# One matrix of the token mixer, v's 1,024 columns, as seven Strassen block products among u's chunks

## The chip, the cores and the metric

The kernel runs on one core of one Trainium2 chip. The metric is the device time of one execution in microseconds (us), lower being better. Five engines matter here: TensorE (PE, with its weight loads PEld), VectorE (DVE), ScalarE (ACT), GpSimd (POOL) and SyncE (SP), whose queue issues most loads.

## What is computed

Two layers of a decoder trunk over 256 tokens of width 1,024, each an FFN, a mixer and a second FFN, all in float32. The part that matters:

```python
def _mixer(x, ...):
    z = x @ w_in
    u, v, q, k, val, gates = jnp.split(z, SPLITS, axis=-1)
    u = jax.nn.gelu(u, approximate=False)
    v = jax.nn.gelu(v, approximate=False)
    h_a = _chunked_sgu(u, v, sgu_ln_g, sgu_ln_b, sgu_w, sgu_b)
    ...                                   # q, k, val -> h_b, by differential attention
    g = jax.nn.sigmoid(gates.reshape(bsz, seq, N_BRANCH, D_MODEL) + gate_b)
    m = g[:, :, 0] * (h_a @ w_branch[0]) + g[:, :, 1] * (h_b @ w_branch[1])
    return m @ w_out

def _chunked_sgu(u, v, g, b, w_s, b_s):
    v = _layernorm(v, g, b)
    ...                                   # 8 groups of 128 columns, chunks of 128 tokens
    s = jnp.einsum('gtr,bnrgc->bntgc', w, vb) + b_s.T[None, None, :, :, None]
    return u * s.reshape(bsz, seq, SGU_WIDTH)
```

So v is one product of x (256 x 1,024) and a 1,024 x 1,024 matrix, followed by a GELU and a layer norm over its columns.

## The kernel before

**Precision by pieces.** Each float32 matrix is split into a high part (ACT copies it into the reduced format float32r) and a low part (DVE subtracts the high part from the original). A product is three passes on PE: high x high, low weights x high, high weights x low. `split` does this for activations; `stream` and `pieces` do it for weights, 128x1024 at a time. The high and low parts of weights live in two pools, `hi` and `lo`, of eight 128x1024 slots each (`HL`). The raw weights arrive by `fetch`, one DMA of 1 MB on SP's queue, into four `raw` slots.

**Two shapes of product.** `gemm_a2` (lines 295 and 302) gives transposed results: weights are stationary, and the high and low parts of x lie side by side as a moving operand of 512 columns; u, q, k and half of the gates use it, one chunk of 256 columns at a time, two weight pieces each. `gemm_b` and `gemm_b2` (through `rows_b` and `three`, line 283) give token rows: x is stationary, a weight piece holds two of the eight k blocks for 512 columns, and the two token blocks of 128 are two PSUM banks. A piece costs six matmuls of 512 columns per token block. val, v and half of the gates use it.

**The mixer's order on PE.** PE's order is that in which the program is written (PE is scheduled by hand); the other engines' instructions are ordered by a scheduler according to priority and readiness, in order once issued. val (`gemm_b2`, during the last steps of the norm before), four pairs of q and k, gates (rows and columns, twice), u's chunks 0 and 1, v in two halves of 512 columns, u's chunks 2 and 3, the branch of attention (`branch_rows(1)`, `branch_columns(1)`), the branch of the gating unit (`branch_rows(0)`, `branch_columns(0)`), and w_out.

**Work beside it.** Attention (`attend`), `settle` (v's norm) and `spatial` (the 128x128 position mixing, a few PE matmuls each, then DVE and ACT) are generators. `beside(task, delay)` starts one after so many beats; `beat(w)` counts them along PE's program: a chunk of `gemm_a2` is 2 beats, a product of 12 matmuls is 1, a half of `gemm_b` is 4. POOL does attention's copies and reciprocal roots, and issues the loads of constants, `wsT` and `bsb` for `spatial` among them.

**Strassen in the FFNs.** The FFNs have such products already: `strassen_sums` makes four sums of blocks of x out of the rows that the norm leaves in `norm.rows` (in place), and splits each; `seven` and `gemm_seven` run seven products of 128x512 by 512x512. Sums of weights come from `plus` (a DVE add, line 359) and `gather` (a DMA on POOL's queue that adds to what is in SBUF, line 353). One product is this, with `x` a sum of x or a block of it:

```python
def product(ps, x, w, start, stop):
    for k in range(4):
        hi, lo = (v[:, k % 2 * 512 : k % 2 * 512 + 512] for v in w[k // 2])
        for n, (y, o) in enumerate(((hi, 0), (lo, 0), (hi, 1))):
            PE.matmul(ps, x[o](k), y, ...)                 # line 376
        beat(0.25)
```

While `line[2]` is set, every weight split and every `plus` is queued behind the one before it on its engine, in the program's order.

Of the kernel before, what the change touches and what calls it, by code (L numbers as in the profile page):

```python
# [12 lines left out]
F32R = mybir.dt.float32r  # L13
# [41 lines left out]
def trunk(ctx, tc, x, xT, w13a, w13b, w2, wb, wqk, wu, wg, wgr, wbr, wbrr, wo, gateb, gatebr, sgug, sgub, sguwT, sgubias, lam, diffg,  # L55
# [48 lines left out]
    def sm(s, n, dtype=F32, bufs=2):  # L104
        return small.tile([P, n], dtype, tag=f"{s}{n}", name=name(s), bufs=bufs)
# [139 lines left out]
    def split(hi, lo, src, eng=V, after=(None, None)):  # L245
        with behind(after[0]):
            a = A.activation(hi, src, AF.Copy).ins  # L247
        with behind(after[1]):
            return a, eng.tensor_tensor(out=lo, in0=src, in1=hi.bitcast(F32), op=ALU.subtract).ins  # L249
# [329 lines left out]
    class Norm:  # L579
# [166 lines left out]
        def close(self):  # L746
# [3 lines left out]
            return self  # L750

    def ffn(l, f, i, norm, last=False):
        xh, xl = parts(both)
# [80 lines left out]

        def strassen_sums(to, made, v11, v21, v12, v22, apart=1):
            to[:] = [tuple(lambda k, v=v: v[:, k * P : (k + 1) * P] for v in m) for m in made]
            for n, (out, a, b, op) in ((0, (v22, v21, v22, ALU.subtract)), (2, (v21, v11, v21, ALU.subtract)),
                                       (1, (v11, v22, v11, ALU.subtract)), (3, (v12, v12, v11, ALU.add))):
                V.tensor_tensor(out=out, in0=a, in1=b, op=op)
                if n in (2, 3):  # L840
                    yield apart
            for n, out in ((0, v22), (2, v21), (1, v11), (3, v12)):
                split(*made[n], out)
                yield apart

        def seven(src, x_sums):

            x11, x12, x22 = (tuple(lambda k, o=o, t=t, h=h: x_cat[h][:, k, o + t * P : o + (t + 1) * P] for o in (0, T))
                             for t, h in ((0, 0), (0, 1), (1, 1)))
            (w11, w21), (w12, w22) = ([v[:, o : o + CH] for o in (0, CH)] for v in src)  # L850
# [92 lines left out]
    def mixer(l, i, norm):  # L943
# [9 lines left out]

        gemm_b2([wb[l, VAL_, 0], wb[l, VAL_, 1]], xh, xl, got_val, norm=norm)

        hb = slots("hb", 2 * KT, F32R)
# [169 lines left out]

        u_part((0, 1))
        vg = [act.tile([P, 2, 512], F32, tag="val", name=name("vg"), bufs=2) for _ in range(NT)]
        vst = [sm("vst", 12, bufs=2) for _ in range(NT)]
        for h in range(2):  # L1130
            def got_v(t, ps, c, n):
                A.activation(vg[t][:, h], ps, AF.Gelu)
                V.bn_stats(out=vst[t][:, h * 6 : h * 6 + 6], in_=vg[t][:, h])
            gemm_b(wb[l, V_, h], KT, xh, xl, got_v)
        def settle():
            for t in range(NT):
                mv = sm("mv", 2)
                V.bn_aggr(out=mv, in_=vst[t])
                r = rsqrt(mv[:, 1:2], EPS)
                for h in range(2):  # L1140
                    s = slice(h * 512, h * 512 + 512)
                    V.scalar_tensor_tensor(out=vg[t][:, h], in0=vg[t][:, h], scalar=mv[:, 0:1], in1=g_bc[:, s],
                                            op0=ALU.subtract, op1=ALU.mult)
                    V.scalar_tensor_tensor(out=vg[t][:, h], in0=vg[t][:, h], scalar=r, in1=b_bc[:, s],
                                            op0=ALU.mult, op1=ALU.add)
                    yield 1

# [29 lines left out]

        beside(settle(), 2.6)
        for gp in range(GROUPS // 2):
            beside(spatial(gp), 7.4 + 1.1 * gp)  # L1180
        u_part((2, 3))

# [149 lines left out]
```

## Time and profile before

| | |
|---|---|
| median of 3 runs | 1189.68 us (1189.35 to 1190.64) |
| profiled execution | 1189.92 us, span of its instructions 1188.2 us |
| granted TensorE clock | 1.000 |
| PE busy | 1180.8 us, 99%, 5771 matmuls |
| DVE, ACT, POOL busy | 85%, 70%, 25% |
| DMA | 276.15 MB, mean 232 GB/s |

How to read the profile's rows: L283 is line 283 of the kernel before; an instruction is given as output<-inputs by the names of tiles, with partitions x elements. A group shows its count, the time in which at least one of it ran, the mean duration of one in ns, and the idle time ahead of it with what ended it. A timeline's row has start and length in us. Matmuls overlap, so their pitch (start to start) counts and not their duration. In the table of windows an engine's column is its busy time in the window, with its count of instructions.

### The profile page before, as it was taken

What the parts mean: (1) busy time and instruction counts of PE and PEld (TensorE: products, weight loads), DVE (VectorE), ACT (ScalarE), POOL (GpSimd) and SP (SyncE); (2) the same over time, 40 slices, a digit from 0 to 9 for tenths busy, and PEclk for the clock granted to TensorE, in tenths of its full rate; (3) what the DMA queues carried; (4) which work ended last, traced back from release to release, by engine and by line L of the source; (5) the groups of instructions that cost most, each with busy time, mean ns of one, the idle gap of its engine ahead of it and who ended that gap; (6) DMA issues with size and microseconds to landing.
All of it is one profiled execution on the core that took longest, in us unless ns stands there. A gap on an engine that the chain in (4) does not pass through costs nothing.

```text
span 1188.2 us, 16675 instructions
## 1 busy us (share of the span) xinstructions
PE 1180.8 (99%) x5771; PEld 993.6 (84%) x5771; DVE 1010.2 (85%) x1558; ACT 828.5 (70%) x1418; POOL 297.3 (25%) x356
## 2 busy tenths in 40 slices
PE   9999999999999999999999999999999999999998
PEld 7888888888888888888888888888888888888887
DVE  6889989888688989889899889888965989988895
ACT  6688667559955677886567877576788556679761
POOL 1211301247420220071020061004564112102510
PEclk9999999999999999999999999999999999999999
DMA  9869976758865658689668699576666755886981
GB/s 348 277 205 265 304 267 206 264 191 222 256 205 181 222 184 274 197 290 263 226 215 267 184 300 275 186 289 233 211 204 207 255 177 172 256 250 211 291 231 36
DMA packets 129797, 276.15 MB, mean 232 GB/s; under 512 B 89088, under 2 KB 90160, under 8 KB 105648
## 3 DMA queue, kind: packets, MB, share of 16 engines
q1 hardware_dynamic: 121968, 248.80, 63.3%
q0 software_dynamic: 7312, 25.76, 9.3%
q8 instruction: 45, 0.74, 0.2%
q10 hardware_dynamic: 432, 0.52, 0.1%
q14 instruction: 40, 0.33, 0.1%
HBM read 249.10 MB, written 1.05 MB: 211 GB/s over the span
## 4 chain that ended last, share of the span: by engine, by line
PE 99%; DMA 1%; DVE 0%; ACT 0%; SPq 0%; issue 0%; ACTq 0%
PE bank L283 46%; PE bank L295 15%; PE sbank L376 12%; PE bank L405 10%; PE bank L302 8%; PE sbank L405 3%; PE bank L516 2%; PE sbank L991 1%; PE bank L376 1%; PE sbank L1047 1%; PE sbank L1165 1%; DMA raw<-in_w13b 1%; PE sbank L1045 0%; PE sbank L685 0%; PE sbank L664 0%; SPq L494 0%
## 5 line engine op out<-in xcount | busy, mean ns | idle before, releaser
L197 DVE TENSOR_TENSOR wlo<-raw,whi 128x1024 fp32r<-128x1024 f32 (+1 forms) x374 | 414.2, 1133 | 59.2 <-ACT whi L195 43.6
L195 ACT ACTIVATE whi<-raw 128x1024 fp32r<-128x1024 f32 (+1 forms) x378 | 353.0, 960 | 130.9 <-PE bank L283 43.7
L283 PE MATMUL bank<-whi,x 128*128 128x512 f32 x1224 | 386.3, 390 | 0.0
L283 PEld LDWEIGHTS bank<-whi,x 128*128 128x128 f32 x1224 | 229.8, 188 | 47.5
L283 PE MATMUL bank<-wlo,x 128*128 128x512 f32 x612 | 238.2, 389 | 0.0
L295 PE MATMUL bank<-x,whi 128*128 128x512 f32 x640 | 153.3, 391 | 0.0
L295 PEld LDWEIGHTS bank<-x,whi 128*128 128x128 f32 x640 | 118.2, 188 | 23.8
L283 PEld LDWEIGHTS bank<-wlo,x 128*128 128x128 f32 x612 | 114.9, 188 | 23.4
L249 DVE TENSOR_TENSOR wlo<-raw,whi 128x1024 fp32r<-128x1024 f32 (+1 forms) x96 | 109.8, 1161 | 16.7 <-ACT whi L247 7.8
L247 ACT ACTIVATE whi<-raw 128x1024 fp32r<-128x1024 f32 (+1 forms) x96 | 92.9, 984 | 41.6 <-DVE raw L359 23.4
L229 POOL COPY seven<-seven 128x512 uint16<-128x512 uint16 x16 | 63.7, 4041 | 108.4 <-ACT whi L195 54.6
L302 PEld LDWEIGHTS bank<-x,wlo 128*128 128x128 f32 x640 | 81.4, 191 | 2.9
L302 PE MATMUL bank<-x,wlo 128*128 128x256 f32 x640 | 82.6, 283 | 0.0
L405 PE MATMUL bank<-whi,hhi 128*128 128x512 f32 (+1 forms) x182 | 68.2, 374 | 0.0
L405 PE MATMUL bank<-whi,hlo 128*128 128x512 f32 (+1 forms) x182 | 67.9, 373 | 0.0
L405 PE MATMUL bank<-wlo,hhi 128*128 128x512 f32 (+1 forms) x182 | 67.9, 373 | 0.0
L967 POOL TENSOR_TENSOR swap<-swap,sin_t 128x512 f32<-128x512 f32 x16 | 27.5, 1716 | 100.6 <-DMA swap<-z 81.6
L728 POOL COPY nvia<-ntwo 128x256 uint16<-128x256 uint16 x20 | 9.6, 527 | 157.6 <-DMA ntwo<-nvia 107.6
L303 ACT ACTIVATE r<-bank 128x256 f32<-128x256 f32 x96 | 34.8, 372 | 16.6 <-PE bank L302 16.5
L359 DVE TENSOR_TENSOR raw<-raw,home 128x1024 f32<-128x1024 f32 x32 | 38.6, 1218 | 4.1 <-DMA home<-in_w13b 4.1
L376 PE MATMUL sbank<-whi,xhs 128*128 128x512 f32 x128 | 42.0, 389 | 0.0
L405 PEld LDWEIGHTS bank<-whi,hlo 128*128 128x128 f32 x182 | 34.3, 188 | 6.1
(283 smaller groups left out, 2154.7 us busy)
## 6 DMA issues: line engine op xcount, KB each, us to landing
raw<-in_w13b SPq DMA_DIRECT2D x68, 1024.0 KB, 5.5
raw<-in_w SPq DMA_DIRECT2D x32, 1024.0 KB, 6.4
raw<-in_wb SPq DMA_DIRECT2D x16, 1024.0 KB, 5.4
raw<-in_wqk SPq DMA_DIRECT2D x16, 1024.0 KB, 5.8
home<-in_w13b SPq DMA_DIRECT2D x16, 512.0 KB, 6.1
raw<-in_w13a SPq DMA_DIRECT2D x8, 1024.0 KB, 4.8
home<-in_w SPq DMA_DIRECT2D x16, 512.0 KB, 5.4
raw<-in_wgr SPq DMA_DIRECT2D x8, 1024.0 KB, 5.1
```

What stands on the lines that cost most here:

```text
L195: inline(A, A.activation(h, r, AF.Copy).ins)
L197: low = eng.tensor_tensor(out=w, in0=r, in1=h.bitcast(F32), op=ALU.subtract).ins
L229: eng.tensor_copy(out=o, in_=i)
L247: a = A.activation(hi, src, AF.Copy).ins
L249: return a, eng.tensor_tensor(out=lo, in0=src, in1=hi.bitcast(F32), op=ALU.subtract).ins
L283: PE.matmul(ps, xx, w, start=start and n == 0, stop=stop and n == 2)
L295: PE.matmul(b[-1], hi[:, k * P : (k + 1) * P], xc(k), start=k == 0, stop=False)
L302: PE.matmul(b[n][:, :T], lo[:, k * P : (k + 1) * P], xc(k)[:, :T], start=False, stop=k == KT - 1)
L303: emptied[0] = A.activation(r[:, s], b[n][:, T:], AF.Copy, scale=scale).ins
L359: inline(V, V.tensor_tensor(out=v, in0=v, in1=m, op=ALU.add).ins)
L376: PE.matmul(ps, x[o](k), y, start=start and k == n == 0, stop=stop and k == 3 and n == 2, skip_group_check=True)
L405: PE.matmul(q[c][t][:, :n] if o == 0 else more[:, :n], x(k, t), y, start=k == 8 and m == 0 and (c, t) != (1, 0), stop=k == FT - 1 and m == ...
```

## The change

v's 96 matmuls per mixer become seven products, 84 matmuls. A 2 x 2 grid of blocks is made of x (token block by half of k) and of the matrix (half of k by half of the columns). Seven products are run one after another in three side banks, `bx`, `bz` and `bq`; `bx` and `bz` go on adding up, and results of the blocks are read out between products (`got_v`). Five of the seven products take their weights from r1 and r2, two raw slots that hold w11 and w12 and then sums: one comes from `plus`, three from `gather`. The products are strung through u's four chunks: u 0, one product, u 1, one, u 2, two, u 3, three. The four sums of x are made right behind val and the norm, and their split parts take two `hi` and two `lo` slots until v ends. `settle` runs per token block, and it and `spatial` start behind the last product, with shorter delays, since no chunk of u comes after v any more. `strassen_sums` moves out of `ffn`, and the x blocks get a helper of their own; neither alters the FFNs.

```diff
@@ -749,6 +749,21 @@
                 x_cat = self.x
             return self
 
+    def strassen_sums(to, made, v11, v21, v12, v22, apart=1):
+        to[:] = [tuple(lambda k, v=v: v[:, k * P : (k + 1) * P] for v in m) for m in made]
+        for n, (out, a, b, op) in ((0, (v22, v21, v22, ALU.subtract)), (2, (v21, v11, v21, ALU.subtract)),
+                                   (1, (v11, v22, v11, ALU.subtract)), (3, (v12, v12, v11, ALU.add))):
+            V.tensor_tensor(out=out, in0=a, in1=b, op=op)
+            if n in (2, 3):
+                yield apart
+        for n, out in ((0, v22), (2, v21), (1, v11), (3, v12)):
+            split(*made[n], out)
+            yield apart
+
+    def x_blocks():
+        return (tuple(lambda k, o=o, t=t, h=h: x_cat[h][:, k, o + t * P : o + (t + 1) * P] for o in (0, T))
+                for t, h in ((0, 0), (0, 1), (1, 1)))
+
     def ffn(l, f, i, norm, last=False):
         xh, xl = parts(both)
         h_hi, h_lo = ([act.tile([P, 512], F32R, tag="slot", name=name(n)) for _ in range(FT // 2)] for n in ("hhi", "hlo"))
@@ -832,21 +847,9 @@
             made = [[home(v) for v in w] for w in (("main", "side"), ("side", "main"), ("main", "slot"), ("side", "slot"))]
             yield from strassen_sums(x_sums, made, t11, t21, t12, t22)
 
-        def strassen_sums(to, made, v11, v21, v12, v22, apart=1):
-            to[:] = [tuple(lambda k, v=v: v[:, k * P : (k + 1) * P] for v in m) for m in made]
-            for n, (out, a, b, op) in ((0, (v22, v21, v22, ALU.subtract)), (2, (v21, v11, v21, ALU.subtract)),
-                                       (1, (v11, v22, v11, ALU.subtract)), (3, (v12, v12, v11, ALU.add))):
-                V.tensor_tensor(out=out, in0=a, in1=b, op=op)
-                if n in (2, 3):
-                    yield apart
-            for n, out in ((0, v22), (2, v21), (1, v11), (3, v12)):
-                split(*made[n], out)
-                yield apart
-
         def seven(src, x_sums):
 
-            x11, x12, x22 = (tuple(lambda k, o=o, t=t, h=h: x_cat[h][:, k, o + t * P : o + (t + 1) * P] for o in (0, T))
-                             for t, h in ((0, 0), (0, 1), (1, 1)))
+            x11, x12, x22 = x_blocks()
             (w11, w21), (w12, w22) = ([v[:, o : o + CH] for o in (0, CH)] for v in src)
             bx, bz, bq = (side_bank() for _ in range(3))
             g0, v0, v1, g1 = (slots("seven", 2)[0] for _ in range(4))
@@ -952,6 +955,12 @@
                     A.activation(val[t][:, h], ps[h], AF.Copy)
 
         gemm_b2([wb[l, VAL_, 0], wb[l, VAL_, 1]], xh, xl, got_val, norm=norm)
+
+        x_sums = []
+        wide = [[p.tile([P, HC], F32R, tag=n, name=name("xhs")) for p, n in ((hi_pool, "hi"), (lo_pool, "lo"))] for _ in range(2)]
+        made = [[v[:, n % 2 * 512 : n % 2 * 512 + 512] for v in wide[n // 2]] for n in range(4)]
+        for _ in strassen_sums(x_sums, made, *(norm.rows[v] for v in ((0, 0), (1, 0), (0, 1), (1, 1)))):
+            pass
 
         hb = slots("hb", 2 * KT, F32R)
 
@@ -1124,26 +1133,67 @@
                 (_, uu), = gemm_a2([wu[l, gp]], both, lambda m: uu)
                 A.activation(uu, uu, AF.Gelu)
 
-        u_part((0, 1))
         vg = [act.tile([P, 2, 512], F32, tag="val", name=name("vg"), bufs=2) for _ in range(NT)]
         vst = [sm("vst", 12, bufs=2) for _ in range(NT)]
-        for h in range(2):
-            def got_v(t, ps, c, n):
-                A.activation(vg[t][:, h], ps, AF.Gelu)
+
+        def seven():
+
+            x11, x12, x22 = x_blocks()
+            (w11, w21), (w12, w22) = ([wb[l, V_, h][:, o : o + CH] for o in (0, CH)] for h in range(2))
+            bx, bz, bq = (side_bank() for _ in range(3))
+            cross = s512("cross")
+
+            def got_v(t, h, src=None):
+                A.activation(vg[t][:, h], vg[t][:, h] if src is None else src, AF.Gelu)
                 V.bn_stats(out=vst[t][:, h * 6 : h * 6 + 6], in_=vg[t][:, h])
-            gemm_b(wb[l, V_, h], KT, xh, xl, got_v)
-        def settle():
-            for t in range(NT):
-                mv = sm("mv", 2)
-                V.bn_aggr(out=mv, in_=vst[t])
-                r = rsqrt(mv[:, 1:2], EPS)
-                for h in range(2):
-                    s = slice(h * 512, h * 512 + 512)
-                    V.scalar_tensor_tensor(out=vg[t][:, h], in0=vg[t][:, h], scalar=mv[:, 0:1], in1=g_bc[:, s],
-                                            op0=ALU.subtract, op1=ALU.mult)
-                    V.scalar_tensor_tensor(out=vg[t][:, h], in0=vg[t][:, h], scalar=r, in1=b_bc[:, s],
-                                            op0=ALU.mult, op1=ALU.add)
-                    yield 1
+
+            product(bq, x12, pieces(fetch(w21)), True, True)
+            A.activation(cross, bq, AF.Copy)
+            yield
+            r1 = fetch(w11)
+            p1 = pieces(r1)
+            r2 = fetch(w12)
+            product(bx, x11, p1, True, False)
+            p1 = pieces(plus(r1, r2))
+            gather(r1, w22)
+            gather(r2, w22)
+            yield
+            V.tensor_tensor(out=vg[0][:, 0], in0=bx, in1=cross, op=ALU.add)
+            got_v(0, 0)
+            product(bz, x_sums[0], p1, True, False)
+            A.activation(vg[1][:, 1], bz, AF.Copy)
+            product(bx, x_sums[1], pieces(r1), False, False)
+            gather(r1, w21)
+            A.activation(vg[0][:, 1], bx, AF.Copy)
+            yield
+            product(bx, x_sums[2], pieces(r2), False, False)
+            V.tensor_tensor(out=vg[1][:, 1], in0=vg[1][:, 1], in1=bx, op=ALU.subtract)
+            got_v(1, 1)
+            product(bz, x_sums[3], pieces(fetch(w22)), False, True)
+            V.tensor_tensor(out=vg[0][:, 1], in0=bz, in1=vg[0][:, 1], op=ALU.subtract)
+            got_v(0, 1)
+            product(bx, x22, pieces(r1), False, True)
+            got_v(1, 0, bx)
+            yield
+
+        line[:] = None, None, True
+        products = seven()
+        for gp in range(GROUPS // 2):
+            u_part((gp,))
+            next(products)
+        line[:] = None, None, False
+
+        def settle(t):
+            mv = sm("mv", 2)
+            V.bn_aggr(out=mv, in_=vst[t])
+            r = rsqrt(mv[:, 1:2], EPS)
+            for h in range(2):
+                s = slice(h * 512, h * 512 + 512)
+                V.scalar_tensor_tensor(out=vg[t][:, h], in0=vg[t][:, h], scalar=mv[:, 0:1], in1=g_bc[:, s],
+                                        op0=ALU.subtract, op1=ALU.mult)
+                V.scalar_tensor_tensor(out=vg[t][:, h], in0=vg[t][:, h], scalar=r, in1=b_bc[:, s],
+                                        op0=ALU.mult, op1=ALU.add)
+                yield 0.8
 
         wsT, bsb = slots("wsT", 4), slots("bsb", 4)
         for h in range(2):
@@ -1175,10 +1225,10 @@
                 split(h[:, :T], h[:, T:], s1[:, j * T : (j + 1) * T])
             yield 0
 
-        beside(settle(), 2.6)
+        for t in range(NT):
+            beside(settle(t), 0.6 + t)
         for gp in range(GROUPS // 2):
-            beside(spatial(gp), 7.4 + 1.1 * gp)
-        u_part((2, 3))
+            beside(spatial(gp), 4.4 + 1.1 * gp)
 
         m_hi, m_lo, turned_rows = [], [], [None, None]
 
```

## The prediction

> **What bounds the kernel now.** I read the page first: busy time by engine, then the chain.
>
> ```profile
> span 1188.2 us, 16675 instructions
> PE 1180.8 (99%) x5771; PEld 993.6 (84%) x5771; DVE 1010.2 (85%) x1558; ACT 828.5 (70%) x1418; POOL 297.3 (25%) x356
> ```
> Busy PE alone proves little, since matmuls overlap. Hence the second view, the waits of PE:
>
> ```profile
> PE bank L516 <- ACT whi L247: 1.7, 1, 1.7
> PE sbank L528 <- DVE warm L524: 1.0, 1, 1.0
> PE sbank L664 <- ACT minus L662: 0.8, 1, 0.8
> ```
> These are all its waits: 3.5 us in 1188.2, two at the start, one in the last norm. In the mixers PE never waits, so a matmul taken out there shortens the run by its pitch, as long as everything else keeps up. Third view, the chain in order of time, around one Strassen product of the FFN, one u-like column group, and v's two stretches in layer 0:
>
> ```profile
> 152.38 2.72 PE sbank L376 x12
> ...
> 215.83 3.65 PE bank L295 x16
> 219.49 1.91 PE bank L302 x16
> ...
> 315.39 6.83 PE bank L283 x30
> 323.55 14.98 PE bank L283 x66
> ```
> A product is 2.72 us, so a matmul's pitch is 0.227. A column group (one u chunk) is 3.65 + 1.91 = 5.56. v is 6.83 + 14.98 = 21.81 for 96 matmuls.
>
> **The change part by part.** *PE.* v goes from 2 halves x 2 token blocks x 8 k x 3 passes = 96 matmuls to 7 products x 12 = 84: 7 x 2.72 = 19.04, a saving of 2.77 us per mixer, 5.5 us in two. Nothing is added on PE. [...]
>
> *Sums of x behind the norm.* Four adds and four splits of 128x512:
>
> ```profile
> L839 DVE TENSOR_TENSOR xf<-nvia,xf x3: 677/678/678, 450.7 to 1037.1; 128x512 f32<-128x512 f32 x3
> L247 ACT ACTIVATE xhs<-nvia x9: 619/634/638, 446.4 to 1042.7; 128x512 fp32r<-128x512 f32 x9
> L249 DVE TENSOR_TENSOR xhs<-nvia,xhs x9: 679/680/684, 453.1 to 1043.7; 128x512 fp32r<-128x512 f32 x9
> ```
> 8 x 0.68 = 5.4 us of DVE and 4 x 0.63 = 2.5 of ACT, once per mixer, off PE's path if the split weights are far enough ahead. How far they are, ACT's timeline against PE's shows (a split, and the first matmul that uses it):
>
> ```profile
> 264.79 2.94 ACT L195 ACTIVATE whi<-raw 128x1024 fp32r<-128x1024 f32 x3
> 277.61 0.45 PE L283 MATMUL bank<-whi,x 128*128 128x512 f32 x1
> ...
> 286.98 1.99 ACT L195 ACTIVATE whi<-raw 128x1024 fp32r<-128x1024 f32 x2
> 302.74 1.55 PE L295 MATMUL bank<-x,whi 128*128 128x512 f32 x6
> ...
> 356.55 1.06 ACT L195 ACTIVATE whi<-raw 128x1024 fp32r<-128x1024 f32 x1 [3.56 <-PE bank L283]
> 375.07 0.40 PE L283 MATMUL bank<-whi,ha 128*128 128x512 f32 x1
> ```
> Following the pieces in order, the first pair is the second gate's first piece (lead 12.8 us, about the lowest between the queries and the branches), the second u's first (15.8), the third the last branch's first, where ACT waits only for PE to free a slot (18.5). So 5.4 us of DVE is hidden, price 0; without cover it would be up to 5.4 per mixer.
>
> *Two of eight hi and lo slots held* from there until v ends. Six slots are four pieces ahead of the two in use. Pieces are used at 5.56/2 = 2.8 us each, so the lead falls by at most 2 x 2.8 = 5.6: 12.8 becomes 7.2 or more. Price 0, bounds 0 and a few us if ACT's bursts of attention grow longer than that.
>
> *The u and v stage.* Its busy time, the next stage's, and two FFN windows with products in them:
>
> ```profile
> 302.74:349.47 46.73, 46.73 (x251) 40.38 (x249) 34.36 (x61) 36.71 (x74) 16.77 (x41) 1.00 0.78 243
> 349.47:375.07 25.60, 25.60 (x147) 22.42 (x145) 22.44 (x40) 12.99 (x22) 0.00 (x0) 1.00 0.48 167
> ...
> 90.00:105.00 15.00, 15.00 (x68) 12.43 (x67) 15.00 (x18) 12.68 (x18) 0.00 (x0) 1.00 0.81 275
> 135.00:150.00 15.00, 15.00 (x68) 12.21 (x67) 15.00 (x16) 9.75 (x11) 1.82 (x3) 1.00 1.01 265
> ```
> (columns PE, PEld, DVE, ACT, POOL). The stage becomes 46.73 - 2.77 = 43.96. Added there, by these rows:
>
> ```profile
> L197 DVE TENSOR_TENSOR wlo<-raw,whi 128x1024 fp32r<-128x1024 f32 (+1 forms) x374 | 414.2, 1133 | 59.2 <-ACT whi L195 43.6
> L195 ACT ACTIVATE whi<-raw 128x1024 fp32r<-128x1024 f32 (+1 forms) x378 | 353.0, 960 | 130.9 <-PE bank L283 43.7
> L359 DVE TENSOR_TENSOR raw<-raw,home 128x1024 f32<-128x1024 f32 x32 | 38.6, 1218 | 4.1 <-DMA home<-in_w13b 4.1
> L1132 ACT ACTIVATE vg<-bank x8: 574/590/600, 325.4 to 925.0; 128x512 f32<-128x512 f32 x8
> L1172 DVE TENSOR_TENSOR sgu<-sgu,u x8: 681/688/693, 362.0 to 960.5; 128x512 f32<-128x512 f32 x8
> L1142 DVE SCALAR_TENSOR_TENSOR vg<-vg,mv,bc x8: 740/743/1049, 338.4 to 930.7; 128x512 f32<-128x512 f32 x8
> ```
> DVE: 6 more low halves (14 pieces for 8) x 1.11 = 6.6, two adds of r1 and r2 x 1.21 = 2.4, three joins of banks x 0.69 = 2.1; less the part of `settle` that leaves the stage, six of eight passes, 6 x 0.74 = 4.4. So 34.36 + 6.7 = 41.1 of 43.96, 93%. ACT: 6 x 0.93 + 3 copies x 0.59 = 7.4, so up to 44.1 of 43.96; but the stage now also splits ahead for the branches:
>
> ```profile
> 302.74:349.47 46.73, 18.17 (x18) 1.00 0.78 243
> ```
> 18 splits fall in it while u and v have 16, the net lead grown there. With six slots at most four pieces are ahead at either end, so 22 are due and none extra: 36.71 + 4 x 0.93 + 1.8 = 42.2, 96%. Tight, but the FFN windows show PE without a gap beside a DVE at 100%, with the same products and two slots lent. Price 0 to 0.3; bounds 0 and the second rival's.
>
> *The gathers.* Three accumulating loads of 1 MB on POOL's queue, six DMAs, ahead of the wsT and bias loads and among attention's POOL steps. Their cost now:
>
> ```profile
> L353 POOL DMA_DIRECT2D raw<-in_w13b x6: 850/872/917, 476.5 to 1064.2; - x6
> DMA to landing us min/median/max: 5.3/6.6/11.5
> ```
> Call T the end of the first product. Then u1 ends at T + 5.6, the w11 product at 8.3, u2 at 13.8, the next product at 16.6, and there the first gathered pieces are due. They follow this chain: the third pair of splits (its slots come free at T, two adds before it) ends about T + 4 to 6, as attention's steps interfere; second half issued 0.9 later; 6.6 to land; 0.9 + 1.1 to split: T + 13.5 to 15.5. It is due 1.4 after the product starts, T + 18. Margin 2.5 to 4.5 us. The second gather has T + 18 + 9.5 = 27.5 against 30.3 + 1.4. ACT's hi copy waits for the landing at its queue's head, and u3's copies (due T + 19.3) and u2's evacuation stand behind it. Price at the median landing 0; at 11.5 see the first rival.
>
> *Order after v.* `settle` and `spatial` now lie under the first branch only. Counted in beats, the last `spatial` falls right before the second branch's rows (before, one column group earlier). Its chain now:
>
> ```profile
> 371.30 1.06 PE L1165 MATMUL sbank<-wsT,vg 128*128 128x128 f32 x8
> 372.98 0.75 DVE L1170 TENSOR_TENSOR sgu<-sbank,bsb 128x256 f32<-128x256 f32 x2
> 375.31 0.42 DVE L249 TENSOR_TENSOR ha<-sgu,ha 128x256 fp32r<-128x256 f32 x1
> ```
> From the matmuls' end at 372.36 to the second low part at about 376.1: 3.7 us. It is used after three pieces of six matmuls, 18 x 0.227 = 4.1. It just fits; I take 0.3 per mixer, bounds 0 and 1. DVE in that window goes from 22.44 to 22.44 + 4.4 of 25.6, over 100%, but its pieces are about 14 ahead and lose at most 1.3 of that.
>
> Sum: -5.5 + 2 x 0.3 = -4.9 against the profiled execution's 1189.92 (span 1188.2 and 1.7 around it), which lies 0.24 above the median 1189.68: 1184.8 as a median. The forecast's own range is 1183.9 (no stall, 5.5 and 0.3 of spread) to 1187.2.
>
> **The rivals.** *Gathers land late.* With 11.5 us instead of 6.6 the first is ready at T + 18.4 to 20.4 against 18, the second as much later: 0.4 to 2.4 and some 0.5 more, about 2.4 per mixer: 1189.68 - 5.5 + 4.8 = 1189.0, no change. For it: attention's transposes run beside. Against: light traffic in v's stretch. The Trainium skill ("SBUF — State Buffer", section "SBUF: two separate sides") states that a load issued from POOL can starve for descriptors while DVE holds the port they share. By that rule a DVE at 93% would push landings to the upper row; the 6.6 median, found beside an FFN DVE at 90 to 100%, speaks against most of it.
>
> *ACT cannot fill its queue (slower).* In the stage ACT idles 46.73 - 36.71 = 10 us now. If half of that stays, since its head waits for gathers, freed slots and bank results, 44.1 + 5 = 49.1 us of queue stand against 43.96; the lead left at the end hides little with six slots, so some 4.5 us per mixer reach PE: 1189.68 - 5.5 + 9 = 1193.2. It turns into a loss from a stall over 2.8 per mixer, measurably from 4. For it: 96 to 100% of ACT in order, dependent on DVE, POOL and DMA. Against: FFN's products, and ACT had 12.8 to 18 us of lead here.
>
> *The change doesn't save PE time*, because products alternate between two banks: 1189.7. The x12 row at 2.72 speaks against it.
>
> **How the numbers follow.** Forecast 0.55; late gathers 0.16 (a quarter of it still faster); ACT 0.23; no saving 0.06. A measurement of this kernel tells about 0.2%, 2.4 us. Faster 0.58, same 0.18, slower 0.24. The range is 1183.9 to 1192.5, leaving out the worse half of the ACT case.
>
> **What would show it.** L283 loses 192 matmuls and L376 gains 168, each x12 still 2.72 us; PE's waits stay near 3.5 us; u's start to the first branch takes 44 us in place of 46.73. A PE wait on ACT whi or DVE wlo before the fourth product means gathers; one before the sixth or seventh product, with ACT busy throughout, means ACT; one on ha means `spatial`. I am wrong if PE waits over 3 us in a mixer anywhere.

## The result, and the profile after

The changed kernel takes 1236.93 us (1236.43 to 1237.46) against 1189.74 for the kernel before on the same chip: ratio 1.0396, interval 1.0378 to 1.0414. It is 47 us slower; the forecast was 5 us faster, and its range ended at 1192.5. The page of the changed kernel, as first shown for before:

```profile
span 1234.9 us, 16749 instructions
PE 1189.8 (96%) x5747; PEld 997.3 (81%) x5747; DVE 1047.5 (85%) x1596; ACT 841.9 (68%) x1444; POOL 313.0 (25%) x368
```

The 24 matmuls are gone (5771 to 5747), yet PE is busy for longer and idle 4% of the span. Its waits in the changed kernel (columns: total us, times, longest):

```profile
PE sbank L376 <- ACT d L1064: 14.5, 2, 7.5
PE sbank L1215 <- DVE vg L1194: 14.2, 3, 6.6
PE sbank L376 <- ACT vg L1167: 6.4, 2, 3.6
PE sbank L376 <- DVE vg L1170: 2.2, 2, 1.2
```

37.3 us in four new groups, all in the mixers: one wait ahead of the fourth product (L376), one ahead of the fifth (L1167 is the copy that empties bank `bx`), a small one ahead of the seventh, and one at `spatial` (L1215), which comes behind v. The windows of the changed kernel for u and v, and then the first branch, in the first mixer and the second (columns PE, PEld, DVE, ACT, POOL, granted clock, DMA share, GB/s):

```profile
303.62:363.44 59.82, 48.66 (x238) 40.78 (x237) 40.08 (x49) 41.97 (x83) 27.46 (x47) 0.91 0.86 225
363.44:397.97 34.53, 27.89 (x145) 23.90 (x144) 30.43 (x63) 16.44 (x24) 0.00 (x0) 0.90 0.51 183
912.20:972.05 59.85, 47.87 (x238) 40.26 (x237) 38.70 (x49) 41.07 (x81) 27.75 (x47) 0.91 0.84 224
972.05:1008.19 36.14, 28.59 (x146) 24.40 (x144) 31.31 (x62) 17.26 (x26) 0.00 (x0) 0.86 0.50 179
```

Before, these stages took 46.73 and 25.60 us in both mixers at a clock of 1.00. So u and v lost 13.1 us twice and the first branch 8.9 and 10.5: 45.7 of the 47. The clock column is new: it is below 1.00 in all four.

**Ahead of the fourth product.** The timeline of the changed kernel there, four engines together (in brackets stands how long the engine was idle before the instruction, and what ended that):

```profile
320.39 3.87 POOL L353 DMA_DIRECT2D raw<-in_wb  x4
...
330.99 0.39 PE L376 MATMUL sbank<-whi,xhs 128*128 128x512 f32 x1
...
332.54 1.06 ACT L247 ACTIVATE whi<-raw 128x1024 fp32r<-128x1024 f32 x1 [9.45 <-DMA raw<-in_wb]
333.63 1.23 DVE L249 TENSOR_TENSOR wlo<-raw,whi 128x1024 fp32r<-128x1024 f32 x1 [8.47 <-ACT whi L247]
335.37 1.06 ACT L247 ACTIVATE whi<-raw 128x1024 fp32r<-128x1024 f32 x1 [1.77 <-DMA raw<-in_wb]
336.46 1.23 DVE L249 TENSOR_TENSOR wlo<-raw,whi 128x1024 fp32r<-128x1024 f32 x1 [1.60 <-ACT whi L247]
337.61 0.68 DVE L1161 TENSOR_TENSOR vg<-sbank,cross 128x512 f32<-128x512 f32 x1
...
338.43 0.76 PE L376 MATMUL sbank<-whi,xhs 128*128 128x512 f32 x1 [7.06 <-ACT d L1064]
```

ACT stands 9.45 us at the head of its queue for a gathered piece, DVE 8.47 us for ACT. Behind DVE's two splits stands L1161, the add that reads `bx`, and the fourth product adds up in `bx`: PE restarts as soon as that add ends. The releaser that the profile names, ACT d, has nothing to do with it.

**Behind v.** The timeline of the changed kernel, DVE's row of v's norm and PE's at `spatial`:

```profile
368.52 0.15 DVE L255 TENSOR_SCALAR ve<-mv 128x1 f32<-128x1 f32 x1
...
376.26 0.46 PE L1215 MATMUL sbank<-wsT,vg 128*128 128x128 f32 x2
...
377.60 1.22 DVE L197 TENSOR_TENSOR wlo<-raw,whi 128x1024 fp32r<-128x1024 f32 x1
378.73 0.21 DVE L261 TENSOR_SCALAR nwy<-nwa,nwy 128x1 f32<-128x1 f32 x1
378.86 1.22 DVE L197 TENSOR_TENSOR wlo<-raw,whi 128x1024 fp32r<-128x1024 f32 x1
379.99 0.27 DVE L260 TENSOR_SCALAR nwa<-nwy,ve 128x1 f32<-128x1 f32 x1
...
382.56 1.41 DVE L1194 SCALAR_TENSOR_TENSOR vg<-vg,nwy,bc 128x512 f32<-128x512 f32 x2
...
383.36 1.65 PE L1215 MATMUL sbank<-wsT,vg 128*128 128x128 f32 x6 [6.64 <-DVE vg L1194]
```

The reciprocal root in `settle` is eight small operations in a chain, one chain for each token block. In the last links of the second block's chain, DVE's order puts a split of 1.2 us between two links: each link takes 0.2 us, and the next comes 1.3 us later. From the first link of the first block to the last passes over v are 14 us, and most of `spatial`'s first matmuls wait for these passes.

### The profile page after: what moved, and what is told of

The parts are those of the page before. It is cut to its first block, busy times and chain, and to the rows that moved or that the text cites. A ratio compares the mean times of both kernels' runs of the same rounds, so it can differ in the third digit from the quotient of the medians.

```text
span 1234.9 us, 16749 instructions
## 1 busy us (share of the span) xinstructions
PE 1189.8 (96%) x5747; PEld 997.3 (81%) x5747; DVE 1047.5 (85%) x1596; ACT 841.9 (68%) x1444; POOL 313.0 (25%) x368
## 4 chain that ended last, share of the span: by engine, by line
PE 88%; DVE 4%; DMA 3%; issue 2%; ACT 1%; POOL 1%; SPq 0%; ACTq 0%; POOLq 0%; DVEq 0%
PE bank L283 39%; PE bank L295 13%; PE sbank L376 12%; PE bank L405 9%; PE bank L302 7%; PE sbank L405 3%; DMA raw<-in_wb 2%; PE bank L516 1%; DVE wlo L197 1%; PE sbank L1000 1%; PE bank L376 1%; PE sbank L1215 1%; DMA raw<-in_wbrr 1%; DMA raw<-in_w13b 1%; DVE wlo L249 1%
## 5 line engine op out<-in xcount | busy, mean ns | idle before, releaser
L197 DVE TENSOR_TENSOR wlo<-raw,whi 128x1024 fp32r<-128x1024 f32 (+1 forms) x358 | 397.4, 1135 | 33.7 <-ACT whi L195 32.0
L195 ACT ACTIVATE whi<-raw 128x1024 fp32r<-128x1024 f32 (+1 forms) x362 | 335.4, 954 | 116.7 <-PE bank L283 30.6
L283 PE MATMUL bank<-whi,x 128*128 128x512 f32 x1096 | 346.2, 390 | 0.0
L283 PEld LDWEIGHTS bank<-whi,x 128*128 128x128 f32 x1096 | 205.7, 188 | 42.9
L283 PE MATMUL bank<-wlo,x 128*128 128x512 f32 x548 | 213.3, 389 | 0.0
L249 DVE TENSOR_TENSOR wlo<-raw,whi 128x1024 fp32r<-128x1024 f32 (+1 forms) x124 | 146.6, 1203 | 41.4 <-ACT whi L247 31.2
L247 ACT ACTIVATE whi<-raw 128x1024 fp32r<-128x1024 f32 (+1 forms) x124 | 121.0, 997 | 61.8 <-DVE raw L359 23.1
L283 PEld LDWEIGHTS bank<-wlo,x 128*128 128x128 f32 x548 | 102.9, 188 | 20.9
L376 PE MATMUL sbank<-whi,xhs 128*128 128x512 f32 x192 | 68.4, 421 | 21.0 <-ACT d L1064 14.5
L229 POOL COPY seven<-seven 128x512 uint16<-128x512 uint16 x16 | 53.5, 3395 | 121.4 <-ACT whi L195 81.7
L376 PEld LDWEIGHTS sbank<-whi,xhs 128*128 128x128 f32 x192 | 39.3, 204 | 30.8 <-ACT d L1064 15.3
L376 PE MATMUL sbank<-whi,x 128*128 128x512 f32 x144 | 47.5, 391 | 2.2 <-DVE vg L1170 2.2
```

The source lines that it names most:

```text
L195: inline(A, A.activation(h, r, AF.Copy).ins)
L197: low = eng.tensor_tensor(out=w, in0=r, in1=h.bitcast(F32), op=ALU.subtract).ins
L229: eng.tensor_copy(out=o, in_=i)
L283: PE.matmul(ps, xx, w, start=start and n == 0, stop=stop and n == 2)
L376: PE.matmul(ps, x[o](k), y, start=start and k == n == 0, stop=stop and k == 3 and n == 2, skip_group_check=True)
```

## The experiments

"Before" below is always the kernel before, run beside the experiment: 1189.5 to 1189.8 us.

### The loads

**Without the three accumulating loads.**

```diff
             p1 = pieces(plus(r1, r2))
-            gather(r1, w22)
-            gather(r2, w22)
...
-            gather(r1, w21)
```

> The three accumulating loads of each mixer are left out, so r1 and r2 keep w11 + w12 and w12, and v's result is not the sum it should be; all products, splits and PE work stay. Theory G (the gathers land late, ACT and DVE wait for them at the head of their queues, and the later waits follow from that backlog): PE's two waits of 7.2 and 7.6 us in the products and the 3 to 3.7 us ahead of the sixth product go, the half-speed clock with them, and the time is 1184 to 1192 us. Theory S (settle and spatial are called too soon behind the last product, by themselves): the 6.8 us waits for settle stay, 1198 to 1206 us. Theory W (ACT and DVE have too much work in the stage): the time stays above 1220 us.

(The waits that this puts at 7.2 and 7.6 us are 7.06 and 7.48 in PE's timeline, and the product that it calls the sixth is the fifth.)

Measured 1212.10 us, ratio 1.0188 (1.0168 to 1.0208), outside the ranges of all three theories. The loads cost 24.8 us, about half of the loss; 22.3 us over before are left without any of them. (r1 and r2 keep what they hold in three products, so v's values are not the reference's.) Its largest waits:

```profile
PE sbank L1212 <- DVE vg L1191: 11.5, 2, 6.6
PE sbank L376 <- DVE vg L1167: 5.3, 2, 2.9
```

The wait at `spatial` is there as in the changed kernel; that at the fourth product is gone.

**Plain loads in their place**, 1 MB each on SP's queue (the sums of weights are not formed).

```diff
-            gather(r1, w22)
-            gather(r2, w22)
+            reload(r1, w22)      # step(); nc.sync.dma_start(raw, more)
+            reload(r2, w22)
...
-            gather(r1, w21)
+            reload(r1, w21)
```

> The changed kernel with its three accumulating loads turned into plain 1 MB loads on SP's queue into the same r1 and r2, at the same places of the program (they overwrite instead of add, so v's sums are not formed; every wait stays). If the slow landing of POOL's accumulating loads (10 to 13 us) is what hurts, plain loads at 5 to 7 us bring most of the 24.8 us that the gathers cost: 1214 to 1222 us. If the dependence itself does (split, load again, split, with ACT and DVE waiting in order), the time stays above 1228 us.

1219.33 us, ratio 1.0251 (1.0230 to 1.0271). The same bytes to the same places cost 7.2 us as plain loads on SP's queue and 24.8 as accumulating ones on POOL's. Two things differ, and this run doesn't part them. First, the loads start sooner. SP issues r1's as soon as the last split of r1's sum is done, at 319.26:

```profile
319.29 0.33 SPq L358 DMA_DIRECT2D raw<-in_wb  x1
```

It lands 4.9 us later. POOL's queue, held up by attention's root, issues r1's two halves at 322.10 and 322.64, behind r2's, and they land 10.4 and 12.6 us later. Second, the loads take less of the DMA engines' time. The DMA view shows this, of the changed kernel (first two rows, 318 to 345 us) and of this run (last two rows, 312 to 345); the columns are packets, MB, share of 16 engines' time:

```profile
q0 software_dynamic: 864, 3.15, 63.5%
q1 hardware_dynamic: 1200, 1.31, 18.4%
```
```profile
q1 hardware_dynamic: 3508, 7.05, 69.5%
q0 software_dynamic: 164, 0.57, 10.1%
```

POOL's queue (q0), in the changed kernel nothing but the six accumulating loads, moved 3.15 MB in 0.635 x 27 = 17.1 us of all engines, 184 GB/s; SP's queue (q1) in this run 7.05 MB in 0.695 x 33 = 22.9 us, 307 GB/s. Whether the adding or POOL's queue makes them slow is not shown: POOL's plain loads of constants in this run (last row) moved 0.57 MB in 0.101 x 33 = 3.3 us, 171 GB/s, while its plain load of 512 KB in the kernel before, between 290 and 305 us, took 0.085 x 15 = 1.3 us, some 410 GB/s.

**The other order of the two gathers.** In the changed kernel r2's gather was issued ahead of r1's, though r1 is used first. Here r2's is put behind r1's:

```diff
-            gather(r2, w22)
+            with behind(gathered[0]):
+                gather(r2, w22)
```

> Only the order of four DMAs on POOL's queue is changed: r1's two halves are issued ahead of r2's. In the changed kernel r2's went first and r1's landed 10.4 and 12.6 us after issue. Theory G with the queue order as its cause: r1 lands 5.6 us sooner, PE's wait in the fourth product falls from 7.2 to under 2.5 us and one spell of half clock per mixer may go; 1236.9 - 2 x (5 to 9) = 1219 to 1227 us. If the wait is due to the transfer of 2 MB as a whole or to DVE's order, under 3 us of gain: 1234 or more.

1241.39 us (1237.44 to 1245.34), ratio 1.0434 (1.0395 to 1.0474): no gain. The wait ahead of the fourth product fell to 4.4 us or less, and others grew:

```profile
PE sbank L378 <- ACT d L1066: 8.3, 2, 4.4
PE sbank L378 <- DVE vg L1173: 7.5, 2, 4.2
```

The longest landing rose to 14.3 us, from 12.6. What is gained at the product that uses r1 is lost again further on: it is not one load that is badly placed.

**The read of `bx` ahead of the gathered pieces on DVE.**

```diff
-            V.tensor_tensor(out=vg[0][:, 0], in0=bx, in1=cross, op=ALU.add)
+            line[1] = V.tensor_tensor(out=vg[0][:, 0], in0=bx, in1=cross, op=ALU.add).ins
```

> One line: the add that empties bank bx (output into vg, an operand of DVE) becomes the head of DVE's chain of splits and sums, so it and nothing gathered stands in front of the fourth product's bank. In the changed kernel that add ran at 337.61, behind both low halves of the first gathered piece (333.63 and 336.46), and PE waited 7.1 us for it. Theory (order on DVE): the fourth product starts when the first half of its own weights is split, about 334.9, and waits again about 1.3 us for the second half: the wait falls from 7.1 to some 3.5 to 5 us, with less time at half clock behind it; 2.2 to 5 us per mixer, 1237 to 1226 to 1232. Rival (the landings alone set it): the wait moves from the bank to the weights and stays at 6 us or more; 1235 to 1238.

1243.87 us, ratio 1.0453 (1.0437 to 1.0469): worse than both expectations. PE's timeline of this run:

```profile
335.01 0.50 PE L376 MATMUL sbank<-whi,xhs 128*128 128x512 f32 x1 [3.90 <-ACT whi L247]
336.27 0.79 PE L376 MATMUL sbank<-wlo,xhs 128*128 128x512 f32 x1 [0.76 <-DVE wlo L249]
...
341.61 0.50 PE L376 MATMUL sbank<-wlo,xhs 128*128 128x512 f32 x1 [2.41 <-DVE wlo L249]
```

3.90 + 0.76 + 2.41 = 7.07, against one wait of 7.06. The add was the last link, and behind it stood the next ones: the weights themselves, then a step of v's statistics that waits for ACT. The theory that DVE's order alone makes this wait is refuted.

### The clock

**PE kept busy through two of the waits**: 28 spare matmuls (`fill`) ahead of the fourth product and of the first `spatial`.

```diff
+            fill(bank())         # 28 x PE.matmul(b, x_cat[0][:, 0, :P], x_cat[0][:, 0], ...)
             product(bx, x_sums[1], pieces(r1), False, False)
...
             b = side_bank()
+            if gp == 0:
+                fill(b)
```

> The changed kernel with 28 spare matmuls of 512 columns (28 x 0.227 = 6.4 us, inputs long there, results unused) ahead of the fourth product and 28 ahead of the first spatial product of each mixer, that is inside the two waits of 7.1 and 6.6 us; the longer PE program does 112 matmuls more. Theory (the clock): after those waits the records show the granted clock at 0.5 for 6.8 us each, 10.2 once, 30.6 us in all, in which half the work is lost, 15.3 us; with PE kept busy the clock stays at 1.00 there and the time falls by 10 to 15 us, to 1222 to 1227, though PE does more. Rival (other engines set the pace there anyway, so a slow PE costs nothing): the clock stays up, but the same time goes into waits a little later, 1234 to 1240. Second rival (the clock falls for another reason, such as load): the half-clock stretches stay, 1237 to 1245.

1233.28 us, ratio 1.0361 (1.0343 to 1.0378): 3.65 us less than the changed kernel's 1236.93, though PE does 112 matmuls more, and far from the 10 to 15 of the theory. The windows of the fourth product, first of the changed kernel, then of this run:

```profile
338.00:341.00 3.00, 2.57 (x6) 2.11 (x7) 1.56 (x3) 3.00 (x12) 2.25 (x6) 0.50 1.02 195
```
```profile
339.00:342.00 3.00, 2.37 (x11) 2.00 (x12) 1.57 (x3) 2.97 (x12) 2.08 (x6) 1.00 1.10 206
```

The clock did stay up. But the next wait grew:

```profile
354.16 0.79 PE L376 MATMUL sbank<-whi,xhs 128*128 128x512 f32 x1 [6.03 <-ACT vg L1172]
```

It was 2.85 us in the changed kernel, on the same copy. So in u and v ACT and its inputs set the pace, and a slow PE between two of its stops costs nearly nothing. The first branch took 32.7 instead of 34.5 us in the first mixer. So with PE kept busy at these two places some 4 us of 47 come back; half clock is a small part of the loss.

### Sums and slots

Three runs on the kernel before: its own order, with the four sums of x, with the four hi and lo slots held until v ends (through copies of one column), and with both.

```diff
+        for _ in strassen_sums(x_sums, made, *(norm.rows[v] for v in ((0, 0), (1, 0), (0, 1), (1, 1)))):
+            pass
...
+        for w in wide:                                   # behind v: this holds the slots
+            for v in w:
+                V.tensor_copy(sm("nwa", 1), v[:, :1].bitcast(F32))
```

> The kernel before with two hi and two lo slots held from the norm until v is done, by four one-column copies that each hold a slot, and no sums. The run with sums and slots cost 6.2 us. If the six slots do it (ACT and DVE run less far ahead, attention's copies fall behind): 1194 to 1197 us. If the 5.4 us of DVE work behind the norm does it: 1189 to 1191 us.

> The kernel before with the sums of x made and split into hi and lo slots that come free at once, so the pieces have all eight slots afterwards. If the slots cost the 6.2 us: 1189 to 1191 us. If the added work does: 1194 to 1197 us.

> The kernel before with the sums of x made behind the norm and their two hi and two lo slots held until v is done, v by the old product. The prediction's price for this part is 0: 1189 to 1191 us. Theory W would have it cost: six slots and 5.4 us more DVE work shorten the lead until PE waits in the gates or at u, 1193 us or more.

Slots alone: 1189.67, ratio 1.0003 (0.9993 to 1.0012), nothing. Sums alone: 1191.43, 1.0017 (1.0007 to 1.0026), some 2 us. Both: 1195.92, 1.0047 (1.0030 to 1.0064), 6 us, more than the two by themselves. The waits that are new in the run with both:

```profile
PE sbank L1051 <- issue: 3.1, 2, 2.2
PE bank L283 <- DVE z L307: 1.6, 2, 0.9
```

L307 writes the result of a group of q and k, L1051 is attention's product with val: both are steps between the norm and u, where the sums come. That the smaller lead of the splits lets the 5.4 us of sums through to these two is likely, since either alone is nearly free, but the step by which it does was not isolated.

### Order and v's norm

**The changed order alone**: v as before, but all four chunks of u ahead of it, `settle` and `spatial` behind it with the new short delays.

```diff
-        u_part((0, 1))
+        u_part((0, 1, 2, 3))
...
-        beside(settle(), 2.6)
+        for t in range(NT):
+            beside(settle(t), 0.6 + t)
...
-            beside(spatial(gp), 7.4 + 1.1 * gp)
-        u_part((2, 3))
+            beside(spatial(gp), 4.4 + 1.1 * gp)
```

> The kernel before with its old v, but with all four chunks of u ahead of v and with settle per block and spatial at the new short delays, under the attention branch alone. Theory S: spatial waits for settle, 5 to 9 us per mixer with some half clock: 1199 to 1210 us. Theory G: DVE is on time without the gathers' backlog, and the order is hidden: 1189 to 1192 us.

1198.87, ratio 1.0077 (1.0057 to 1.0097): the order by itself costs 9 us, 5.6 of it in waits at `spatial` for v's norm.

**No gathers, u's chunk 3 behind the products**, `settle` at 1.2 + 1.5 t and `spatial` at 6.2 + 1.1 gp.

> The changed kernel without its three gathers (v's sums are not formed) and with u's last chunk moved behind the seven products as cover, settle and spatial called 0.6 to 1.8 beats later. Against 1212.1 without gathers. Theory S: the 6.8 and 5.1 us waits for settle and one spell of half clock per mixer go, 1212 - 2 x (6 to 9) = 1194 to 1200 us. If DVE's backlog decides, the waits stay: 1206 us or more.

1206.47, ratio 1.0143 (1.0122 to 1.0163), 5.6 better than without gathers alone and short of theory S. With a chunk behind v the wait at `spatial` shrinks to 2.9 us in all, but without one between the products that at the bank copy grows to 6.4 and 6.7. One cover can't serve both.

**No loads and no sums**, blocks of x in place of the sums:

> The changed kernel without its three accumulating loads and without the four sums of x: the products that used a sum use a block of x, no hi or lo slot is held, and v's values are not those of the reference. Beside the run without the loads alone (1212.1) it gives the price of sums and slots in the changed order. Theory (prices add up): 6 us as in the kernel before with sums and held slots (1195.9 against 1189.7): 1205 to 1207. Rival (they hide behind the other waits of the changed order): 1210 to 1213. Second rival (six slots starve ACT while products and u's chunks alternate): far more than 6, 1195 to 1202.

1208.62, ratio 1.0158 (1.0143 to 1.0173). Sums and slots cost 3.5 us in the changed order, between the theory's 6 and nothing.

**The same with the products in v's old place**, old delays, u's chunks 2 and 3 behind:

> As the run without loads and sums, but the products stand where v's halves stood: u 0, a product, u 1, the other six in a row, the norm of v in one task with its old delay, u 2 and u 3, spatial with its old delays. It leaves the loads and sums out, so v's values are not the reference's. Theory (PE's saving is real, and the loss without loads and sums comes from the order behind v): 5.5 us saved, less the reads of banks that now stand between products without a chunk of u, 1 to 2 us per mixer: 1184 to 1189. Rival (reading banks through full ACT and DVE queues is the loss wherever the products stand): PE waits of 3 us or more between the products, 1195 to 1205.

1212.03, ratio 1.0188 (1.0171 to 1.0205). Both theories miss: the waits between products are 1.8 us and less, and still `spatial` waits with the old order, over 5 us in each mixer:

```profile
PE sbank L1209 <- DVE vg L1188: 10.3, 2, 5.2
PE sbank L376 <- ACT vg L1158: 3.6, 2, 1.8
```

So the new order is not needed for a loss behind v: with the old one, too, something between v's last product and `spatial` takes too long. That led to the next two.

**The changed kernel without the reciprocal root** in v's norm, one operation in place of eight:

```diff
-            r = rsqrt(mv[:, 1:2], EPS)
+            r = sm("ve", 1)
+            V.tensor_scalar(out=r, in0=mv[:, 1:2], scalar1=EPS, scalar2=None, op0=ALU.add)
```

> The changed kernel with the reciprocal root of v's norm left out: one small operation on DVE in place of eight per token block (v is scaled by its variance, so its values are not the reference's). In the changed kernel the eight operations of 0.14 to 0.27 us stand in a chain, and DVE's order puts a 1.2 us split between two links; from the first link at 368.52 to the last pass at 382.56 are 14 us, and spatial's second product waits 6.64 us for it. Theory (the length of that chain is the loss behind v): the last pass ends near 375, spatial does not wait, and the clock does not fall behind it: 2 x (6.6 + 3.4) = 20 us off, 1217, at least 12. Rival (DVE is simply full in this stretch, so the same work ends as late): the wait moves to a later spatial product or to the second branch, 1230 to 1237.

1222.79, ratio 1.0282 (1.0265 to 1.0299): 14.1 us off. The first branch in this run, both mixers:

```profile
367.37:392.85 25.48, 25.48 (x145) 22.34 (x144) 25.48 (x47) 14.69 (x22) 0.00 (x0) 1.00 0.66 229
966.91:992.83 25.92, 25.92 (x146) 22.65 (x144) 25.92 (x44) 15.30 (x22) 0.00 (x0) 0.98 0.63 226
```

25.5 and 25.9 us: as before the change, with DVE at 100% of the window and PE without a gap. DVE being full is thus no loss; the length of the chain is. (The run also takes 14 links of some 0.2 us, about 3 us of work, off DVE in each mixer, but the branches gain 9.1 and 10.2.) The two branches give 19.3 us, of which 14.1 show in the time; u and v took longer in this run (62.3 us in the first mixer, its wait at the fourth product 7.95).

**One root for both token blocks, on POOL**, as attention makes its own; `settle` becomes one task over both blocks:

```diff
-            r = rsqrt(mv[:, 1:2], EPS)
+            r = rsqrt4(mv, EPS, ALU.add)     # mv of both blocks in one 128x4 tile; eps added on POOL
```

> The changed kernel with one reciprocal root for both token blocks, made on POOL in the way attention's are (14 operations on 128x4), which has no other work in that stretch. Attention's chains on POOL took 6.3 and 10.3 us there, so from 367.5 the root comes at 374 to 378 and the four last passes at 376 to 381, not 383.9. Theory (the chain's length is the loss behind v): the wait of 6.6 us falls to 0 to 4 us: 1220 to 1231. Rival (DVE full): 1233 to 1238.

1228.23, ratio 1.0325 (1.0309 to 1.0340): 8.7 us off with the whole computation kept, inside the theory's range. The chain took 367.66 to 373.97 on POOL, without a split between its links, and the wait at `spatial` fell to 1.1 us.

**No loads, no sums, no root**: what the change is without its three losses.

> The changed kernel without the accumulating loads, without the sums of x (blocks of x in their place) and without the reciprocal root of v's norm; v's values are not the reference's. What is left of the change is PE's 24 matmuls fewer, the products strung through u's chunks, and the order behind v. Theory (the three are the losses, apart from bank reads between products): from 1208.6 the 9 us per mixer that went with the root, so the second branch 25.6 us behind the first as before, and 1189 to 1192: the 5.5 us saved are used up by waits of 1.0 to 1.5 us ahead of the fifth and the seventh product. Rival (there is a further loss in the order): the second branch stays 28 us or more behind the first, 1196 to 1204.

1190.82, ratio 1.0010 (1.0000 to 1.0019). Its waits in products, without one of 0.3 us, and the window of u and v:

```profile
PE sbank L376 <- ACT vg L1158: 2.6, 2, 1.4
PE sbank L376 <- DVE vg L1161: 2.0, 2, 1.0
```
```profile
302.56:349.37 46.81, 44.64 (x238) 38.12 (x237) 37.42 (x49) 41.07 (x82) 19.99 (x41) 1.00 0.73 214
```

PE is busy 44.64 us where 43.96 were forecast; 2.2 us of waits, nearly all for bank reads, make it 46.81, and before it was 46.73. The saving is real, 2.1 us per mixer, and reading the banks between products takes it all back.

Read from here upwards, this is the account: 1190.8; with the root 1208.6 (+17.8); with sums and slots 1212.1 (+3.5); with the loads 1236.9 (+24.8). Out of another order the prices differ (the root is worth 14.1 in the full kernel). No version came out ahead of the kernel before, and none is likely along this path: with the costly parts left out altogether it only draws level.

## Why the prediction was wrong

Two terms failed above all: the gathers, whose wait was put at 0 with 6.6 us to land, and the order behind v, put at 0.3 us per mixer. All terms follow, in the order of the prediction.

- **PE's saving**: near the forecast. A product is 2.75 us from start to start where nothing interrupts it (310.54 to 313.29 in the changed kernel, 2.72 forecast), and 2.1 us of PE's time per mixer were saved where 2.77 were forecast. But that the bank reads between products cost nothing was assumed without a price: 2.2 us per mixer in the run without the three losses.
- **Sums at price 0**: too low. It was worked out from the splits' lead, sums and slots each on its own. Together they cost 6 us in the old order and 3.5 in the new; the bound given there, 5.4 per mixer, holds.
- **Busy time in u and v**: 41.1 for DVE and 42.2 for ACT were forecast, 40.1 and 42.0 measured (38.7 and 41.1 in the second mixer), and the stage is 59.8 us, not 44. The terms were right and the reading of them wrong: 93 and 96% was taken to mean that the stage fits. ACT then stood idle 9.5 us in a row behind one landing, and DVE 8.5.
- **Gathers, price 0**: the main failure in size, 24.8 us. The chain for r1 left out that r2 is free first and shares the queue. With T = 313.29, POOL issued r2's first half at 320.39, T + 7.1, and r1's second half fourth, at T + 9.4, where T + 4.9 to 6.9 were forecast. Then came "6.6 to land", a median over loads in other company. Here four accumulating loads of 512 KB stand one behind another; they landed 6.4, 8.2, 10.4 and 12.6 us after their issues, and r1 was split at T + 24.4, where T + 13.5 to 15.5 were forecast and T + 18 needed. The row of L353 between 318 and 345 us, and a window in it, both of the changed kernel:

```profile
L353 POOL DMA_DIRECT2D raw<-in_wb x6: 857/1048/1616, 320.4 to 338.0; - x6
...
DMA to landing us min/median/max: 6.1/7.6/12.6
```
```profile
326.00:331.00 5.00, 5.00 (x32) 4.42 (x30) 0.00 (x0) 0.00 (x0) 0.00 (x0) 1.00 1.06 202
```

 The first rival had the cause, late gathers, but at 2.4 us per mixer. It took the maximum of the old row as the worst case, though that row holds no two gathers at once, and counted only the wait for the weights. The trace of before could have given the price. Its DMA view from 475 to 492 us, where POOL's queue carries one gather of 1 MB in an FFN:

```profile
q0 software_dynamic: 288, 1.05, 36.7%
```

 That is 0.367 x 17 = 6.2 us of all engines for one gather, so r1's and r2's together take some 12.5 us with nothing else beside them, an estimate from this row. The Trainium skill ("SBUF — State Buffer", section "SBUF: two separate sides") has a POOL load starve while DVE holds their shared port. The window from 326 to 331 us speaks against that as the cause here: for 5 us DVE does nothing at all, the DMA engines' share is 1.06, and they move 202 GB/s. They are full, not starved.
- **Order behind v, 0.3 us per mixer**: the first branch, where `settle` and `spatial` now lie, lost 8.9 and 10.5 in the changed kernel, and the order alone cost 9 us in all. I priced the last `spatial` and its use, and took `settle` for covered because DVE's splits were 14 us ahead. What had to be followed is the chain of `settle` itself, and the trace of before had it (DVE's timeline, and the window from the first row to the end of the last):

```profile
338.09 0.21 DVE L1138 BATCH_NORM_AGGREGATE mv<-vst 128x2 f32<-128x12 f32 x1
...
354.80 1.41 DVE L1144 SCALAR_TENSOR_TENSOR vg<-vg,nwy,bc 128x512 f32<-128x512 f32 x2
```
```profile
338.09:356.21 18.12, 18.12 (x96) 15.62 (x96) 18.08 (x42) 9.13 (x15) 0.94 (x2) 1.00 0.77 276
```

 18 us from the first block's statistics to the last pass, on a DVE that was busy for 18.08 of them while PE didn't wait, hidden by two chunks of u of 5.5 us each and the start of the branch. The change takes those chunks away, and `spatial` now comes 12.8 us behind v's last product (363.44 to 376.26).
- **ACT cannot fill its queue**, the slower rival, had the direction and the mechanism (its head waits for gathers), at 4.5 us per mixer; the stage lost 15.9 against its forecast. Its wait was priced from ACT's mean idle time before, and not from what one late landing holds up on ACT, DVE and PE in turn.
- **The signs named**: L283 and L376 moved as said; PE waited 7.5 us where I had set 3 as the mark for being wrong; a wait before the fourth product meant the gathers, though PE waited there for the read of a bank and not for a weight. The wait at `spatial` and the lower clock were not among the signs.

## What to carry to other kernels

When work that hides a chain is moved away, measure the chain from its first input to its last output in the trace of before: small dependent operations on an in-order engine take as long as what is queued between them, and neither the engine's busy share nor the lead of its other work shows that. A median time to landing holds for loads in the company in which it was measured; several loads queued at once are to be summed, at the rate that their own queue shows (here 184 GB/s for POOL's accumulating loads, 307 for SP's plain ones). A share of 96% busy in a stage is a claim that nothing in it ever waits.

## What the runs showed of the hardware

Before, the granted clock was 1.00 throughout. In the changed kernel it fell to 0.50 in or behind each long wait of PE. Behind that of 7.06 us:

```profile
341.00:343.00 2.00, 2.00 (x6) 1.51 (x6) 2.00 (x6) 0.17 (x1) 1.64 (x5) 0.50 1.00 190
343.00:346.00 3.00, 3.00 (x15) 2.43 (x14) 1.02 (x1) 0.43 (x2) 2.08 (x6) 0.99 0.36 75
```

It stayed there for 4.6 us of matmuls, from 338.4 to 343.0. The wait of 2.85 us ahead of the fifth product was enough too:

```profile
354.00:356.50 2.50, 2.50 (x7) 1.93 (x7) 2.50 (x3) 2.31 (x4) 0.84 (x1) 0.50 1.02 305
```

With waits of up to 1.44 us, in the run without the three losses, the clock stayed at 1.00. The Trainium skill ("TensorE: Matmul & The Clock Gate", section "What's actually happening") gives about 3.4 us of idleness as what halves the clock, and as much work as what restores it. The trace agrees on the effect; the 2.85 us of this case are less than that figure.

By the DMA views above, POOL's accumulating loads moved 184 GB/s of the DMA engines' time where SP's plain loads moved 307. Whether this comes from the adding or from the queue was not tried; POOL's plain loads of constants moved 171 GB/s in one view and some 410 in another.
